# Eight of sixteen K tiles of an attention output projection's last two column blocks by seven products

## The chip, the cores and the metric

The kernel runs on one core of a Trainium2 chip. The metric is device time in microseconds (us) of one execution. The kernel before takes 2151.49 us (median of 3 runs, 2151.38 to 2151.53). All durations below come from one profiled execution of it.

## The reference, cut to what matters

The model is a two-layer encoder trunk over 256 positions of width 2048, float32 throughout. Layer 0 mixes by pooling and attention, layer 1 by an mLSTM, and each layer ends in a gated feed-forward network (FFN). The change touches only the output projection of layer 0:

```python
mixed = jnp.concatenate([pool_out, att_out], axis=-1) @ w_out_ab[e]   # (256, 2048) @ (2048, 2048)
x = x + mixed
x = x + conv_ffn(rms_norm(x, norm_ffn[layer]), ...)
```

The concatenation has 16 K tiles of 128 channels: 4 of pooling, then one for each of 12 heads. The next RMS norm needs all four 512-wide column blocks of `x`.

## The kernel before

**Precision.** Every float32 operand is held as a high part in the matmul's format (F32R) and a low part, the rest. A product is three matmuls: high by high, high by low, low by high. TensorE (PE) runs them all from `mm` (L296).

**The weight stream.** Weights arrive in chunks of 128 partitions by 1024 floats (512 KB), in one fixed order, `Stream`. A chunk is loaded by SyncE's DMA queue (SPq, L101) into one of seven raw buffers `w`. Then ScalarE (ACT) casts it to the high part (L167), and VectorE (DVE) subtracts to get the low part (L168). Both land in one of five buffers `hl`. `Stream.next` keeps loads up to six and splits up to three chunks ahead of the one that PE takes, in program order. Some chunks of the FFNs are first added up on DVE; their kind says how:

```python
    if kind == "sum":
        pin(add(r, r, l))          # L151
    ...
    if kind == "left":
        pin(add(l, l, r))          # L155
    if kind == "chain":
        pin(add(l, l, self.sum))   # L157
        pin(add(r, r, l))          # L158
```

`l` and `r` are the two 512-wide halves of the chunk. These additions are pinned in program order (`pin`), and `split` calls the additions of chunk i ahead of its cast, and those of chunk i + 1 right behind the subtraction of chunk i.

**The output projection.** `out_proj` accumulates each column block `b` (512 columns) in one pair of PSUM banks, for the two halves `t` of the positions. A chunk holds two K tiles of one column block and gives PE 12 matmuls of 512 columns: two K tiles, two halves, three terms. Blocks 0 and 1 run first, interleaved with the end of attention; blocks 2 and 3 then take 8 chunks each. `residual` (L470) adds a finished block into `x`, and `norm.add(b)` follows: squares on ACT (L369), four groups of four transposes on PE (`xt`, L347), and their scaled high and low parts on ACT (L359) and DVE (L362). The FFN's first products `up` need the last block's parts.

**Seven products elsewhere.** In the FFNs, groups of four column tiles already run as a Strassen-like scheme: seven products of sums of blocks in place of eight, in `quads`. There its chunks alternate with ordinary `up` and `dn` chunks.

**What sets the order.** PE's order is that of the program text, with small tasks woven in by an estimated clock (`Weave`). DVE, ACT and SPq are ordered at build time by a scheduler; engines then wait for each other by semaphores. Meanwhile `make_step` builds sums of weights for the FFN in DRAM (`G`), by DMAs that add, from SPq and GpSimd's queue (POOL); each step hangs on the number of a loaded chunk (`places`).

Of the kernel before, what the change touches and what calls it, by code (L numbers as in the profile page):

```python
# [9 lines left out]
F32 = mybir.dt.float32  # L10
# [6 lines left out]
P = 128  # L17
# [48 lines left out]
class Stream:  # L66
# [182 lines left out]
def trunk(ctx: ExitStack, tc: tile.TileContext, gx, xT, xn, call, catt, cml, weights, make, out):  # L249
# [45 lines left out]
    def mm(out_, lhsT, rhs, start, stop):  # L295
        pe.matmul(out_, lhsT, rhs, start=start, stop=stop, skip_group_check=True)  # L296
# [122 lines left out]
    def mov_part(ps, act, kts, first, last):  # L419
# [3 lines left out]
        for i, k in enumerate(kts):  # L423
# [9 lines left out]
            wv.tick(1.29)  # L433

    def mov_group(act, name, width=512, before=None, after=None):

        ps = mmp.tile([P, 2, 512 if width > 256 else width], F32, tag="mm", name=name)
        per = CH * P // width
        hl = None
        for k in range(KT):  # L440
            if k % per == 0:
                before and before(k)
                hl = st.next()
                after and after(k)
# [26 lines left out]

    def out_proj(cat, norm, name, parts, ready):

        pss = [mmp.tile([P, 2, 512], F32, tag="mm", name=f"op{name}_{i}") for i in range(2)]
        for i, kts in enumerate(parts):
            ready(i)
            for ps in pss:
                mov_part(ps, cat, kts, i == 0, i == len(parts) - 1)
        for b in range(NB):
            if b >= 2:  # L480
                ps = mmp.tile([P, 2, 512], F32, tag="mm", name=f"op{name}_{b}")
                mov_part(ps, cat, sum(parts, []), True, True)
            else:
                ps = pss[b]
            residual(ps, b)
            norm.add(b)


    def attention_layer(norm, nxt):
        with ExitStack() as es:  # L490
# [262 lines left out]
            need = [set(range(8)), {"pool0", "pool1"}, set(range(8, 12))]  # L753

            def ready(i):
                wv.until(lambda: need[i] <= done)

            out_proj(cat, nxt, "0", ATT_PARTS, ready)


# [212 lines left out]
    def ffn_layer(layer, norm, nxt):  # L973
        with ExitStack() as es:
# [64 lines left out]

            def product(bank, act, w, c, first, last):  # L1040

                (xh, xl), (wh, wl) = act, (w[:, j, c : c + 512] for j in range(2))
                mm(bank, xh, wh, first, False)
                mm(bank, xh, wl, False, False)
                mm(bank, xl, wh, False, last)
                wv.tick(0.68)

            def block_of(k, t):
# [173 lines left out]
def _mov(w):  # L1222

    return w.reshape(-1, 2, P, 512).transpose(0, 2, 1, 3).reshape(-1, P, CH * P)
# [256 lines left out]
```

## Time and profile before

| | |
|---|---|
| median of 3 runs | 2151.49 us |
| the profiled execution | 2151.58 us |
| its span, first to last instruction | 2149.8 us |
| TensorE clock granted | 1.0 |
| PE busy | 2143.8 us |
| DVE busy | 1792.6 us |
| ACT busy | 1335.6 us |
| DMA | 647.54 MB, mean 301 GB/s |

The span leaves 1.8 us of the profiled time around it. The part that the change touches is block 2 and block 3 of the projection, which PE works on from about 210 to 256 us after the span's start. A row of the timeline gives start and duration in us, engine, line, operation, the tile written, the tiles read, shapes and count; in brackets stands the idle time before it and what ended it. A busy PE row covers the pipeline's depth too, so the pace of matmuls is read from starts, not from the duration of one.

### The profile page before, as it was taken

What the parts mean: (1) busy time and instruction counts of PE and PEld (TensorE: products, weight loads), DVE (VectorE), ACT (ScalarE), POOL (GpSimd) and SP (SyncE); (2) the same over time, 40 slices, a digit from 0 to 9 for tenths busy, and PEclk for the clock granted to TensorE, in tenths of its full rate; (3) what the DMA queues carried; (4) which work ended last, traced back from release to release, by engine and by line L of the source; (5) the groups of instructions that cost most, each with busy time, mean ns of one, the idle gap of its engine ahead of it and who ended that gap; (6) DMA issues with size and microseconds to landing.
All of it is one profiled execution on the core that took longest, in us unless ns stands there. A gap on an engine that the chain in (4) does not pass through costs nothing.

```text
span 2149.8 us, 30986 instructions
## 1 busy us (share of the span) xinstructions
PE 2143.8 (100%) x10752; PEld 1813.8 (84%) x10752; DVE 1792.6 (83%) x2514; ACT 1335.6 (62%) x1872; POOL 243.6 (11%) x304
## 2 busy tenths in 40 slices
PE   9999999999999999999999999999999999999999
PEld 7888888888888888889888888888888888888887
DVE  7686698989889797877888887779898898988985
ACT  7665566766567576656455554456675776766863
POOL 0222111111111111100000011110111111100000
PEclk9999999999999999999999999999999999999999
DMA  9989899999999999968899999997999999988882
GB/s 355 253 225 256 252 252 358 308 340 322 304 328 316 349 325 338 322 178 278 349 339 327 334 303 333 313 319 216 346 317 333 341 335 323 350 291 263 289 271 98
DMA packets 213728, 647.54 MB, mean 301 GB/s; under 512 B 26586, under 2 KB 28930, under 8 KB 206914
## 3 DMA queue, kind: packets, MB, share of 16 engines
q1 hardware_dynamic: 181280, 590.68, 76.5%
q0 software_dynamic: 29216, 51.14, 15.1%
q10 hardware_dynamic: 3074, 3.75, 0.9%
q8 instruction: 84, 1.38, 0.3%
q14 instruction: 74, 0.61, 0.1%
HBM read 616.05 MB, written 131.12 MB: 348 GB/s over the span
## 4 chain that ended last, share of the span: by engine, by line
PE 97%; DVE 2%; issue 0%; DMA 0%; ACT 0%; ACTq 0%; DVEq 0%
PE dn L296 22%; PE p L296 21%; PE up L296 20%; PE op L296 8%; PE mk L296 4%; PE mq L296 4%; PE mo L296 4%; PE mv L296 4%; PE qproj L296 3%; PE kproj L296 1%; PE pool L296 1%; PE vproj L296 1%; PE tr L1118 1%; DVE hl L168 1%; PE qk L296 1%; PE end L296 1%
## 5 line engine op out<-in xcount | busy, mean ns | idle before, releaser
L168 DVE TENSOR_TENSOR hl<-w,hl 128x1024 fp32r<-128x1024 f32 (+1 forms) x916 | 1104.7, 1219 | 253.6 <-ACT hl L167 246.0
L167 ACT CAST hl<-w 128x1024 fp32r<-128x1024 f32 (+2 forms) x915 | 948.7, 1048 | 585.2 <-PE dn L296 113.3
L296 PE MATMUL dn<-hl,g 128*128 128x512 f32 x2064 | 491.5, 391 | 0.0
L296 PE MATMUL up<-xx,hl 128*128 128x512 f32 (+1 forms) x2560 | 466.5, 337 | 0.0
L296 PEld LDWEIGHTS up<-xx,hl 128*128 128x128 f32 x2560 | 405.0, 188 | 63.7
L296 PEld LDWEIGHTS dn<-hl,g 128*128 128x128 f32 x2064 | 385.2, 188 | 79.2
L296 PE MATMUL p<-hl,sx 128*128 128x512 f32 x1152 | 304.2, 390 | 0.2 <-DVE hl L168 0.2
L296 PEld LDWEIGHTS p<-hl,sx 128*128 128x128 f32 x1152 | 212.2, 188 | 42.1 <-DVE hl L168 0.5
L296 PE MATMUL p<-hl,xx 128*128 128x512 f32 x864 | 236.3, 391 | 0.0
L139 POOL DMA_DIRECT2D G<-in_q x140 | 118.4, 852 | 657.6 <-DMA G<-in_q 650.0
L296 PEld LDWEIGHTS p<-hl,xx 128*128 128x128 f32 x864 | 158.2, 188 | 30.1
L143 POOL DMA_DIRECT2D G<-G x124 | 108.2, 872 | 550.8 <-DMA G<-in_q 231.2
L296 PE MATMUL mv<-hl,xx 128*128 128x512 f32 (+2 forms) x480 | 92.4, 350 | 0.0
L296 PE MATMUL mq<-xx,hl 128*128 128x512 f32 (+1 forms) x512 | 91.9, 337 | 0.0
L296 PE MATMUL mk<-xx,hl 128*128 128x512 f32 (+1 forms) x512 | 91.8, 338 | 0.0
L296 PE MATMUL op<-hl,cat 128*128 128x512 f32 x384 | 91.6, 393 | 0.0
L296 PE MATMUL mo<-hl,xx 128*128 128x512 f32 x384 | 90.4, 391 | 0.0
L296 PE MATMUL op<-hl,mcat 128*128 128x512 f32 x384 | 89.7, 392 | 0.0
L296 PEld LDWEIGHTS mq<-xx,hl 128*128 128x128 f32 x512 | 79.2, 188 | 11.6
L296 PEld LDWEIGHTS mk<-xx,hl 128*128 128x128 f32 x512 | 78.8, 188 | 11.4
L296 PEld LDWEIGHTS mv<-hl,xx 128*128 128x128 f32 x480 | 78.1, 189 | 11.1
L296 PEld LDWEIGHTS op<-hl,mcat 128*128 128x128 f32 x384 | 71.4, 188 | 14.6
(250 smaller groups left out, 1939.5 us busy)
## 6 DMA issues: line engine op xcount, KB each, us to landing
w<-in_dn SPq DMA_DIRECT2D x176, 512.0 KB, 6.9
w<-in_up SPq DMA_DIRECT2D x160, 512.0 KB, 6.7
w<-in_m_in SPq DMA_DIRECT2D x124, 512.0 KB, 6.4
w<-G SPq DMA_DIRECT2D x88, 512.0 KB, 7.2
w<-in_q SPq DMA_DIRECT2D x80, 512.0 KB, 7.5
G<-in_q SPq DMA_DIRECT2D x124, 256.0 KB, 7.4
G<-G POOLq DMA_DIRECT2D x124, 256.0 KB, 7.7
w<-in_q SPq DMA_DIRECT2D x120, 256.0 KB, 6.2
```

The costliest lines, as they stand in the source:

```text
L139: pin(add.dma_start(G[r, 0:512], src[r, 512:1024], accum_op=ALU.add))
L143: pin(add.dma_start(G[:, at : at + 512], G[:, of : of + 512], accum_op=ALU.add))
L167: (self.nc.vector.tensor_copy if i + c == 0 else self.nc.scalar.copy)(hl[:, 0, c : c + n], w[:, c : c + n])
L168: self.nc.vector.tensor_sub(hl[:, 1, c : c + n], w[:, c : c + n], hl[:, 0, c : c + n].bitcast(F32))
L296: pe.matmul(out_, lhsT, rhs, start=start, stop=stop, skip_group_check=True)
L1118: pe.transpose(tr[:, j, t * P : t * P + P], src[:, c : c + P], ident)
```

## The change

K tiles 0 to 7 (pooling and heads 0 to 3) of column blocks 2 and 3 no longer go block by block. Four pairs of K tiles, two halves of positions and two column blocks form 2 by 2 block products, each done in seven products (`into`). Their seven results accumulate in four single PSUM banks (b1, b5, b6, b4) and are added straight into `x` by nine additions and one copy (L484 to L488, L496, L503 to L506 of the new program). K tiles 8 to 15 stay as they were.

- PE: 84 matmuls take the place of 96, all of 512 columns.
- The weights come as 4 "sum" and 4 "chain" chunks, 2 plain ones and 4 "left" ones, where 8 plain chunks were: 14 for 8. The 8 sum and chain chunks carry 6 matmuls each, the 2 plain ones 6 each, the 4 left ones 6 each.
- DVE and ACT: `cat_sums` forms the four sums of blocks of `cat` with their high and low parts, four times, in the buffers of `kt` and `vt`; it is queued once all heads are done or on their way.
- Order: block 2's other 8 tiles, its residual, then the 8 sum and chain chunks, one plain chunk of block 3, the rest of the seven products, `norm.add(2)`, and the last three chunks of block 3. So block 2's norm moves from ahead of block 3 to its middle.
- The steps of `make_step` from chunk 76 on shift by the six new chunks.

```diff
--- before.py
+++ after.py
@@ -432,6 +432,80 @@
                 mm(ps[:, t], xl, wh, False, last and i == n - 1)
             wv.tick(1.29)
 
+    def product(bank, act, w, c, first, last):
+
+        (xh, xl), (wh, wl) = act, (w[:, j, c : c + 512] for j in range(2))
+        mm(bank, xh, wh, first, False)
+        mm(bank, xh, wl, False, False)
+        mm(bank, xl, wh, False, last)
+        wv.tick(0.68)
+
+    def pair_sums(two, tv, raw, dst):
+
+        v.tensor_add(tv, two[:, :, 0, :].bitcast(F32), two[:, :, 1, :].bitcast(F32))
+        a11, a21, a12, a22 = (tv[:, k, t * P : t * P + P] for k in range(2) for t in range(2))
+        s1, s2, s3, s4 = (raw[:, j] for j in range(4))
+        v.tensor_sub(s1, a21, a22)
+        v.tensor_add(s3, a11, a21)
+        v.scalar_tensor_tensor(s2, s1, -1.0, a11, ALU.mult, ALU.subtract)
+        v.tensor_sub(s4, s3, a12)
+        v.tensor_sub(s4, s4, a22)
+        for js, hi, lo in dst:
+            a.copy(hi, raw[:, js])
+            v.tensor_sub(lo, raw[:, js], hi.bitcast(F32))
+
+    def into(b, two, sum_of, m, name, apart, room):
+
+        def xs(t, n):
+            return x[:, t, (b + n) * 512 : (b + n + 1) * 512]
+
+        def bank(j):
+            return psp.tile([P, 512], F32, tag="ps", name=f"h{j}_{name}", side=int(j in (1, 5)))
+
+        def block_of(k, t):
+            return [two(k // 2)[:, k % 2, i, t * P : t * P + P] for i in range(2)]
+
+        for q in range(2 * m):
+            p, second = (q % m, q >= m) if apart else (q // 2, q % 2)
+            ends = p == 0, p == m - 1
+            hl = st.next()
+            if not second:
+                if p == 0:
+                    b1, b5 = bank(1), bank(5)
+                product(b1, block_of(2 * p, 0), hl, 0, *ends)
+                product(b5, sum_of(0, p), hl, 512, *ends)
+            else:
+                if p == 0:
+                    b6, b4 = bank(6), bank(4)
+                product(b6, sum_of(1, p), hl, 0, *ends)
+                product(b4, block_of(2 * p + 1, 1), hl, 512, *ends)
+            if q == 2 * m - 1:
+                ca = room()
+                a.copy(ca, b1)
+                v.tensor_add(xs(1, 1), xs(1, 1), b5)
+                v.tensor_sub(xs(0, 1), xs(0, 1), b6)
+                v.tensor_add(xs(1, 0), xs(1, 0), b4)
+                v.tensor_sub(xs(0, 1), xs(0, 1), ca)
+            yield
+        for n in range(m // 2):
+            hl = st.next()
+            for e in range(2):
+                p = 2 * n + e
+                product(b1, block_of(2 * p + 1, 0), hl, e * 512, False, p == m - 1)
+            if n == m // 2 - 1:
+                v.tensor_add(xs(0, 0), xs(0, 0), b1)
+            yield
+        for p in range(m):
+            hl = st.next()
+            product(b6, sum_of(2, p), hl, 0, False, p == m - 1)
+            product(b5, sum_of(3, p), hl, 512, False, p == m - 1)
+            if p == m - 1:
+                v.tensor_add(ca, ca, b6)
+                v.tensor_sub(xs(0, 1), xs(0, 1), b5)
+                v.tensor_add(xs(1, 1), xs(1, 1), ca)
+                v.tensor_sub(xs(1, 0), xs(1, 0), ca)
+            yield
+
     def mov_group(act, name, width=512, before=None, after=None):
 
         ps = mmp.tile([P, 2, 512 if width > 256 else width], F32, tag="mm", name=name)
...
@@ -469,17 +543,33 @@
             xs = x[:, t, b * 512 : b * 512 + 512]
             v.tensor_add(xs, xs, ps[:, t])
 
-    def out_proj(cat, norm, name, parts, ready):
+    def out_proj(cat, norm, name, parts, ready, half=None):
 
         pss = [mmp.tile([P, 2, 512], F32, tag="mm", name=f"op{name}_{i}") for i in range(2)]
         for i, kts in enumerate(parts):
             ready(i)
             for ps in pss:
                 mov_part(ps, cat, kts, i == 0, i == len(parts) - 1)
+        rest = [k for k in sum(parts, []) if half is None or k >= 8]
         for b in range(NB):
             if b >= 2:
                 ps = mmp.tile([P, 2, 512], F32, tag="mm", name=f"op{name}_{b}")
-                mov_part(ps, cat, sum(parts, []), True, True)
+                if half is not None and b == 2:
+                    mov_part(ps, cat, rest, True, True)
+                    residual(ps, b)
+                    wv.until(lambda: norm.blocks == 2)
+                    unit = half()
+                    for _ in range(8):
+                        next(unit)
+                    continue
+                if half is not None:
+                    mov_part(ps, cat, rest[:2], True, False)
+                    for _ in unit:
+                        pass
+                    norm.add(2)
+                    mov_part(ps, cat, rest[2:], False, True)
+                else:
+                    mov_part(ps, cat, rest, True, True)
             else:
                 ps = pss[b]
             residual(ps, b)
...
@@ -752,10 +842,32 @@
                 wv.add(pool_group(stat_group(xx, list(range(KT)), f"pool{g2}"), g2))
             need = [set(range(8)), {"pool0", "pool1"}, set(range(8, 12))]
 
+            sx = []
+
+            def two(p):
+                return catb[0][:, 2 * p : 2 * p + 2]
+
+            def cat_sums():
+                sx.extend(kp.tile([P, 2, 4, 2, P], F32R, tag=tag, name=f"sx{tag}") for tag in ("kt", "vt"))
+                for p in range(4):
+                    tv = t1p.tile([P, 2, S], F32, tag="qt20", name=f"cs{p}")
+                    raw = tp.tile([P, 4, P], F32, tag="tb", name=f"cr{p}")
+                    pair_sums(two(p), tv, raw, [(slice(2 * i, 2 * i + 2), sx[i][:, :, p, 0], sx[i][:, :, p, 1])
+                                                for i in range(2)])
+                    yield 3.5
+                done.add("sums")
+
             def ready(i):
                 wv.until(lambda: need[i] <= done)
-
-            out_proj(cat, nxt, "0", ATT_PARTS, ready)
+                if i == 2:
+                    wv.add(cat_sums())
+
+            def half():
+                wv.until(lambda: "sums" in done)
+                return into(2, two, lambda j, p: [sx[j // 2][:, j % 2, p, i, :] for i in range(2)], 4, "op0", False,
+                            lambda: t1p.tile([P, 512], F32, tag="qt21", name="ca0"))
+
+            out_proj(cat, nxt, "0", ATT_PARTS, ready, half)
 
 
     def mlstm_layer(norm, nxt):
...
@@ -1234,12 +1338,23 @@
     return np.concatenate(out + [some(sum(parts, []), c) for c in range(1024, D, 512)])
 
 
+def _half_chunks(t):
+
+    t = t.reshape(-1, 2, P, 2, 512).transpose(0, 1, 3, 2, 4)
+    b11, b12, b21, b22 = (t[:, k, n] for k in range(2) for n in range(2))
+    return (np.concatenate([b11, b12, b22, b21], axis=2), np.concatenate([b21[0::2], b21[1::2]], axis=2))
+
+
 def _att_chunks(w_in, w_out):
     pool_w, q_w = 512, HEADS * HD
     cols = [pool_w + q_w, pool_w, pool_w + q_w + 512, pool_w + 512, pool_w + 1024]
     a = [_mov(w_in[:, c : c + 512]) for c in cols]
     a += [_stat(w_in[:, c : c + 256], range(KT)) for c in (0, 256)]
-    return np.concatenate(a), _out_chunks(w_out, ATT_PARTS)
+    out = _out_chunks(w_out, ATT_PARTS)[: 2 * KT // 2]
+    rest = [k for k in sum(ATT_PARTS, []) if k >= 8]
+    t = w_out.reshape(KT, P, D)
+    out = [out] + [_mov(t[rest][:, :, c : c + 512].reshape(len(rest) * P, 512)) for c in (1024, 1536)]
+    return np.concatenate(a), np.concatenate(out), *_half_chunks(t[:8][:, :, 1024:].reshape(8 * P, 1024))
 
 
 def _ml_chunks(w_in, w_out):
...
@@ -1458,11 +1573,14 @@
     n = 3 * (MD + 32)
     vg = [t["m_g"][:, c : min(c + n, m_g.shape[1])] for c in range(0, m_g.shape[1], n)]
     pairs = [_pairs(l, t[f"q{l}"]) for l in range(2)]
-    att, ml = chunks("a_in") + chunks("a_out"), vg + chunks("m_in") + chunks("m_out")
+    ao, four, last = (chunks(n) for n in ("a_out", "a_four", "a_last"))
+    ao = (ao[:20] + [e for q in four for e in (("sum", q[:, 0:1024]), ("chain", q[:, 1024:2048]))] + ao[20:21] + last
+          + [("left", q[:, 512:1536]) for q in four] + ao[21:])
+    att, ml = chunks("a_in") + ao, vg + chunks("m_in") + chunks("m_out")
     weights = att + ffn(0)
-    places = [[(24 + 13 * k // 2, 3) for k in range(8)] + [(76 + 9 * k, 4) for k in range(8)]
-              + [(150 + 4 * k, 2) for k in range(8)] + [(180 + 10 * k, 5) for k in range(8)]
-              + [(264 + 8 * k, 4) for k in range(8)]]
+    places = [[(24 + 13 * k // 2, 3) for k in range(8)] + [(82 + 9 * k, 4) for k in range(8)]
+              + [(156 + 4 * k, 2) for k in range(8)] + [(186 + 10 * k, 5) for k in range(8)]
+              + [(270 + 8 * k, 4) for k in range(8)]]
     at = len(weights) + len(ml)
     early = [(at - 240 + 11 * k, 5) for k in range(7)]
     late = [(at - 64 + 9 * k, 4) for k in range(7)]
```

The first place is DVE's queue where block 2 begins. `w` is a raw chunk, `hl` a split one, `x` the residual, `xx` the norm's parts, `op_2` block 2. Before:

```order
L168 TENSOR_TENSOR hl_2066<-w_2009,hl_2066 128x1024
L168 TENSOR_TENSOR hl_2083<-w_2026,hl_2083 128x1024
L470 TENSOR_TENSOR x<-x,op_0_1669 128x512 x2
L168 TENSOR_TENSOR hl_2105<-w_2044,hl_2105 128x1024
L168 TENSOR_TENSOR hl_2135<-w_2064,hl_2135 128x1024
L470 TENSOR_TENSOR x<-x,op_1_1670 128x512 x2
L168 TENSOR_TENSOR hl_2152<-w_2081,hl_2152 128x1024
L168 TENSOR_TENSOR hl_2191<-w_2098,hl_2191 128x1024
L362 SCALAR_TENSOR_TENSOR xx_131<-xt_0_2161,gcol,xx_131 128x256 x2
L168 TENSOR_TENSOR hl_2226<-w_2133,hl_2226 128x1024
```

Now, from the first summed chunk (hl_2203) on:

```order
L151 TENSOR_TENSOR w_2107<-w_2107 128x512
L544 TENSOR_TENSOR x<-x,op_1_1670 128x512 x2
L168 TENSOR_TENSOR hl_2203<-w_2107,hl_2203 128x1024
L157 TENSOR_TENSOR w_2124<-w_2124,w_2107 128x512
L158 TENSOR_TENSOR w_2124<-w_2124 128x512
L168 TENSOR_TENSOR hl_2244<-w_2124,hl_2244 128x1024
L151 TENSOR_TENSOR w_2171<-w_2171 128x512
L362 SCALAR_TENSOR_TENSOR xx_131<-xt_0_2214,gcol,xx_131 128x256
L362 SCALAR_TENSOR_TENSOR xx_131<-xt_2_2229,gcol,xx_131 128x256
L168 TENSOR_TENSOR hl_2271<-w_2171,hl_2271 128x1024
L157 TENSOR_TENSOR w_2201<-w_2201,w_2171 128x512
L362 SCALAR_TENSOR_TENSOR xx_131<-xt_0_2214,gcol,xx_131 128x256
```

Plain subtractions have become a sequence in which additions (L151, L157, L158) stand between one chunk's subtraction and the next.

The second place is DVE's queue at the four "left" chunks (hl_2413 to hl_2456), behind the last plain one (hl_2390), in the changed program:

```order
L168 TENSOR_TENSOR hl_2390<-w_2354,hl_2390 128x1024
L155 TENSOR_TENSOR w_2366<-w_2366 128x512
L488 TENSOR_TENSOR x<-x,ca_2400 128x512
L168 TENSOR_TENSOR hl_2413<-w_2366,hl_2413 128x1024
L155 TENSOR_TENSOR w_2377<-w_2377 128x512
L496 TENSOR_TENSOR x<-x,h_op_2305 128x512
L168 TENSOR_TENSOR hl_2431<-w_2377,hl_2431 128x1024
L155 TENSOR_TENSOR w_2388<-w_2388 128x512
L168 TENSOR_TENSOR hl_2443<-w_2388,hl_2443 128x1024
L155 TENSOR_TENSOR w_2407<-w_2407 128x512
L168 TENSOR_TENSOR hl_2456<-w_2407,hl_2456 128x1024
```

Each subtraction is followed by the next chunk's addition, which its own cast waits for.

The third place is PE's queue around block 2's transposes (`xt_8`, `xt_10`). Before, they stood in block 3's second chunk:

```order
L296 MATMUL op_2_2132<-hl_2226,cat_333 128x512 x12
L296 MATMUL op_2_2132<-hl_2243,cat_333 128x512 x12
L296 MATMUL op_3_2320<-hl_2261,cat_332 128x512 x12
L296 MATMUL op_3_2320<-hl_2282,cat_332 128x512 x6
L347 MATMUL xt_8_2350<-cst,x 128x128 x4
L296 MATMUL op_3_2320<-hl_2282,cat_332 128x512 x6
L347 MATMUL xt_10_2365<-cst,x 128x128 x4
L296 MATMUL op_3_2320<-hl_2299,cat_333 128x512 x12
L296 MATMUL op_3_2320<-hl_2324,cat_333 128x512 x12
```

Now they stand behind the seven products' last chunk (hl_2456), one and a half chunks on:

```order
L296 MATMUL h_op_2321<-hl_2456,sxvt 128x512 x3
L296 MATMUL h_op_2306<-hl_2456,sxvt 128x512 x3
L296 MATMUL op_3_2406<-hl_2470,cat_333 128x512 x12
L296 MATMUL op_3_2406<-hl_2481,cat_333 128x512 x6
L347 MATMUL xt_8_2538<-cst,x 128x128 x4
L296 MATMUL op_3_2406<-hl_2481,cat_333 128x512 x6
L347 MATMUL xt_10_2553<-cst,x 128x128 x4
L296 MATMUL op_3_2406<-hl_2492,cat_333 128x512 x12
```

And DVE's queue from that chunk's subtraction on, where `x` gets its last additions (L504 to L506), which these transposes read:

```order
L168 TENSOR_TENSOR hl_2456<-w_2407,hl_2456 128x1024
L168 TENSOR_TENSOR hl_2470<-w_2429,hl_2470 128x1024
L168 TENSOR_TENSOR hl_2481<-w_2441,hl_2481 128x1024
L503 TENSOR_TENSOR ca_2400<-ca_2400,h_op_2321 128x512
L504 TENSOR_TENSOR x<-x,h_op_2306 128x512
L168 TENSOR_TENSOR hl_2492<-w_2454,hl_2492 128x1024
L168 TENSOR_TENSOR hl_2511<-w_2465,hl_2511 128x1024
L505 TENSOR_TENSOR x<-x,ca_2400 128x512
L506 TENSOR_TENSOR x<-x,ca_2400 128x512
L168 TENSOR_TENSOR hl_2529<-w_2479,hl_2529 128x1024
```

The additions have two chunks' subtractions ahead of them on one side and two in their middle.

More of the change, by code (lines that the diff above doesn't have):

```diff
@@ L1038, in sums @@
                         yield 2.0
[L1040 to L1046, printed above, removed]
             def block_of(k, t):
@@ L1432 @@
     m_g = np.concatenate([wv0, wgate], axis=2).reshape(P, KT * (MD + 32))
-    a_in, a_out = _att_chunks(i["w_in_ab"][0], i["w_out_ab"][0])
+    a_in, a_out, a_four, a_last = _att_chunks(i["w_in_ab"][0], i["w_out_ab"][0])
     m_in, m_out = _ml_chunks(i["w_in_c"][0], i["w_out_c"][0])
@@ L1439 @@
         "call": call, "catt": catt, "cml": cml, "m_g": m_g,
-        "a_in": a_in, "a_out": a_out, "m_in": m_in, "m_out": m_out,
+        "a_in": a_in, "a_out": a_out, "a_four": a_four, "a_last": a_last, "m_in": m_in, "m_out": m_out,
     }
```

## The prediction

> **What bounds the kernel now.** I read the page's busy times and clock first, then the chain of work that ended last, then the stretch that is changed.
>
> ```profile
> span 2149.8 us, 30986 instructions
> PE 2143.8 (100%) x10752; PEld 1813.8 (84%) x10752; DVE 1792.6 (83%) x2514; ACT 1335.6 (62%) x1872; POOL 243.6 (11%) x304
> PEclk9999999999999999999999999999999999999999
> PE 97%; DVE 2%; issue 0%; DMA 0%; ACT 0%; ACTq 0%; DVEq 0%
> ```
>
> PE is busy throughout at the full granted clock, and 97% of the chain is PE. So a matmul removed is worth its time, if PE stays fed; DVE at 83% is the nearest rival. In the changed stretch the chain is PE alone:
>
> ```profile
> 199.91 14.06 PE op L296 x62
> 213.97 0.44 PE xt L347 x4
> 219.89 17.74 PE op L296 x78
> 239.88 16.38 PE op L296 x72
> ```
>
> ```profile
> L296 PE MATMUL op<-hl,cat 128*128 128x512 f32 x384 | 91.6, 393 | 0.0
> ```
>
> These are pieces of the chain by start, length and count. 16.38 / 72 is 0.2275 us a matmul, so a chunk of 12 takes 2.73 us and a chunk of 6 takes 1.36. No piece of another engine stands between. Four transposes take 0.44. By the group's row one matmul lasts 0.39 from start to end, so its end lies 0.17 behind the start of the next.
>
> What feeds PE is cast and subtraction. Two rounds of the timeline, ACT then DVE:
>
> ```profile
> 225.42 1.05 ACT L167 CAST hl<-w 128x1024 fp32r<-128x1024 f32 x1 [1.30 <-PE op L296]
> 226.51 1.22 DVE L168 TENSOR_TENSOR hl<-w,hl 128x1024 fp32r<-128x1024 f32 x1 [1.10 <-ACT hl L167]
> 228.18 1.05 ACT L167 CAST hl<-w 128x1024 fp32r<-128x1024 f32 x1 [1.71 <-PE op L296]
> 229.27 1.22 DVE L168 TENSOR_TENSOR hl<-w,hl 128x1024 fp32r<-128x1024 f32 x1 [1.54 <-ACT hl L167]
> ```
>
> The casts wait for PE to leave a buffer `hl`: splitting is as far ahead as five buffers allow, four chunks ready while a fifth is being made. From cast to subtraction takes 1.09 us (226.51 - 225.42), and both rest more than 1 us in each 2.76 us round. That rest is what the change can spend.
>
> **The saving.** 96 matmuls of 512 columns become 84 of the same shape. The products of the FFN, which have the new ones' form, run at the same pace:
>
> ```profile
> 2070.74 4.08 PE p L296 x18
> 2077.54 1.36 PE p L296 x6
> ```
>
> 4.08 / 18 is 0.2267. Twelve fewer matmuls save 12 x 0.227 = **2.7 us**.
>
> **What a summed chunk costs.** The one place of the trace with a "left" addition between two subtractions and nothing else on DVE:
>
> ```profile
> 496.15 1.23 DVE L168 TENSOR_TENSOR hl<-w,hl 128x1024 fp32r<-128x1024 f32 x1 [0.47 <-ACT hl L167]
> 497.30 0.69 DVE L155 TENSOR_TENSOR w<-w 128x512 f32<-128x512 f32 x1
> 498.15 1.05 ACT L167 CAST hl<-w 128x1024 fp32r<-128x1024 f32 x1 [2.03 <-DVE w L155]
> 499.23 1.23 DVE L168 TENSOR_TENSOR hl<-w,hl 128x1024 fp32r<-128x1024 f32 x1 [1.25 <-ACT hl L167]
> ```
>
> Subtraction, addition, cast and next subtraction form a closed chain, since additions are pinned right behind the subtraction before. From subtraction to subtraction it takes 499.23 - 496.15 = 3.08 us. A back-to-back subtraction frees DVE after 1.15 (497.30 - 496.15), and ACT starts 0.16 after the addition's end. A "sum" or "left" chunk thus takes 3.08 us to make. A "chain" chunk has a second addition that needs the first's result; the trace has no clean case, so I add one whole addition:
>
> ```profile
> L158 DVE TENSOR_TENSOR w<-w 128x512 f32<-128x512 f32 x8 | 5.5, 689 | 0.1
> ```
>
> That gives 3.08 + 0.69 = 3.77 us (between 3.68, if the two overlap as independent ones do, and 3.85, if a full 0.08 for the hand-over comes on top). PE uses such a chunk in 1.36 us. In the FFN 12 or 16 other matmuls follow each; here the eight stand in a row, and so do the four.
>
> **The eight sum and chain chunks.** Let t be the time since PE begins block 2. Then a fifth buffer comes free and chunk one is cast: 0.17 for PE's last matmul to end, 0.16 for the hand-over to ACT, 1.09 to the subtraction, which so starts at 1.4. Seven steps follow: four chain chunks and three sum chunks, 4 x 3.77 + 3 x 3.08 = 24.3. In that queue also stand eight parts of the norm and two residual additions:
>
> ```profile
> 218.06 2.05 DVE L362 SCALAR_TENSOR_TENSOR xx<-xt,gcol,xx 128x256 fp32r<-128x256 f32 x4
> 269.64 0.69 DVE L1030 SCALAR_TENSOR_TENSOR v<-v 128x512 f32<-128x512 f32 x1
> 270.24 0.69 DVE L1031 TENSOR_TENSOR v<-v 128x512 f32<-128x512 f32 x1
> ```
>
> They take 0.5 and 0.6 us each (2.05 / 4; 270.24 - 269.64). Where they lie in ACT's cast (1.2 us with its hand-over) they are free. Not so in the second chain chunk: three parts stand between its additions (1.5), and two parts and two additions behind them (2.2, of which 1.2 free). I take 1.9 of these 2.5, since the first of the parts runs while its own transposes are awaited. The last of the eight is subtracted from 1.4 + 24.3 + 1.9 = 27.6 to 28.8. PE could use it earlier: 48 matmuls of block 2 (10.9), 16 transposes (1.8), seven chunks (9.5) and the first matmul (0.2), together 22.4. So PE loses 28.8 - 22.4 = **6.4 us** there.
>
> **The four left chunks.** From the last chain subtraction's start, DVE has three more subtractions (with its own, 4 x 1.15), two additions into `x` (1.2), then addition, hand-over, cast and subtraction of the first left chunk (0.69 + 0.16 + 1.08 + 1.23): 9.0. (The two additions wait for nothing then.) PE, released 1.2 after that start, has 5 matmuls, 12 + 6 + 6 and one more, 29 x 0.227 = 6.6: it is there at 7.8 and loses 1.2. Each of the three others is made in 3.08 and used in 1.36: 1.7 lost, 5.2 together. Sum **6.4 us**.
>
> **Block 2's transposes.** The order puts them behind the last left chunk by 18 matmuls, and the two L506 additions that they need behind it by four subtractions and three additions. From the last left subtraction's start, DVE is done with these at 5 x 1.15 + 4 x 0.6 + 0.1 = 8.2; PE gets there at 1.2 + 23 x 0.227 = 6.4. Lost: **1.8 us**. What is late next is `xx` of block 2, which only `up` reads, 18 matmuls and block 3's transposes later; I cost that at nothing.
>
> **Sums of `cat`.** Four rounds on DVE, each one 512-wide addition (0.6), five 128-wide operations and two 256-wide ones:
>
> ```profile
> 262.79 0.47 DVE L388 TENSOR_SCALAR dg<-cst,re_n 128x128 f32<-128x128 f32 x2
> 150.00:178.00 28.00, 28.00 (x161) 24.40 (x161) 23.36 (x41) 20.28 (x46) 12.29 (x15) 1.00 0.85 207
> 178.00:190.00 12.00, 12.00 (x62) 10.10 (x61) 6.72 (x9) 5.45 (x8) 2.39 (x3) 1.00 0.95 232
> 178.00:256.30 78.30, 78.30 (x365) 65.01 (x364) 45.12 (x51) 39.51 (x56) 12.92 (x16) 1.00 0.92 264
> ```
>
> In these rows of stretches the fourth and fifth times are DVE's and ACT's. With 0.24 for a 128-wide operation (0.47 / 2) and 0.5 for a 256-wide one, a round is 0.6 + 1.2 + 1.0 = 2.8 us, 11 in all. From 178 to 190 DVE rests 5.3 us and from 190 to 205 again nearly half, so they hide. One risk: heads 10 and 11 still finish there, and a round ahead of their `pt` in DVE's queue holds up PE's `ov`. Between 0 and one round (2.8), I take **0.5**, near the free end, as rest is plenty.
>
> **Six more loads.** 6 x 0.524 MB = 3.1 MB.
>
> ```profile
> DMA packets 7499, 22.45 MB, mean 267 GB/s; under 512 B 1007, under 2 KB 1007, under 8 KB 7494
> q1 hardware_dynamic: 5702, 19.23, 67.5%
> ```
>
> Both rows are of the 84 us from 178 to 262. At 264 GB/s the 78.3 us before moved 20.7 MB; now 23.8 MB go in some 90 us, 264 GB/s again: the stalls themselves make the room. I take zero. If nothing hid them they would cost 3.1 x 0.675 x 84 / 19.23 = 9.3 us, the upper bound.
>
> **Sum.** -2.7 + 6.4 + 6.4 + 1.8 + 0.5 = **+12.4 us**. On the profiled execution's 2151.58 that is 2164.0; on the median, 0.1 lower, 2163.9. I forecast **2163.9 us**, slower. Its own uncertainty: 0.1 either way on each of ten steps, the parts' 1.9 (0 to 2.5), `cat` 0 to 2.8, which makes 2160.5 to 2167.8.
>
> **The rivals.**
> - *The work hides (faster).* If splitting ran far enough ahead, only the saving stayed: 2148.8. For it speaks the rest of over 1 us in each round. Against it: the head start is four chunks of 2.73, 10.9 us, and the eight lag by 7 x about 2.1. It decides where the eight are made in (28.8 - 6.4 - 4.5) / 7 = 2.6 us each or less, the left ones in 1.4. Chance 5%.
> - *Only busy time counts (no change).* DVE has 45.1 us in the 78.3; added are 16 additions (9.6), six subtractions (6.9), 11 for `cat`, nine additions into `x` (5.4): 78.0, against PE's 75.6. If queue order let DVE run dense, the stretch would take 78: 2151.2. Against it: the closed chain leaves DVE idle during each cast. Chance 5%.
> - *Half of it.* If the scheduler's order lets the eight chunks start earlier than I read, only left chunks and transposes count: -2.7 + 6.4 + 1.8 = +5.5, 2157.0. Chance 8%.
> - *Loads late.* SPq's additions into `G` share its queue; with the bound above, 2163.9 + 9.3 = 2173.2. Chance 9%.
> - *The clock falls.* In the left chunks PE would work 1.36 of 3.08 us. At half the clock six matmuls take 2.73, still under 3.08; up to block 3's end 36 matmuls could run slow, 36 x 0.227 = 8.2: between 2163.9 and 2172.1. Every clock digit of the page is 9, and no idle forecast is over 2.4 us (3.77 - 1.36). Chance 5%. The Trainium skill, "TensorE: Matmul & The Clock Gate", section "A second HAM failure mode: psum-queue depth-cycling", tells of a kernel whose frequent short idle gaps made the clock swing between half and full; no trace here has such gaps yet.
>
> The forecast has 68%. The range **2157 to 2170** holds it, half of the half case and part of the two slow ones. About 0.2%, 4.3 us, is what a measurement here can tell from no change. Faster by more, under 2147.2: 2%, as the hiding case is only 2.7 us under the median and a third of it may fall lower. Within: 11% (the other 3% of it, the busy-time case's 5%, and 3% of the half case, whose 2157.0 lies 1.2 over the bound of 2155.8). Slower: the remaining 87%.
>
> **What would show it.** Right: PE idle before single matmuls of the seven products, ended by DVE's L168 or ACT's L167; additions L155 and subtractions in a 3.1 us beat at the left chunks; an idle of about 2 us before `xt`; total about 15 us of PE idle between 205 and 270 us, none new later. Wrong: PE solid there (hiding); casts there that wait for DMA (loads); clock digits under 9. A wrong beat of the chain steps would move both 6.4 together.

## The result and the profile after

The changed kernel takes **2163.52 us** (median of 6 runs, 2162.92 to 2164.96) against 2151.51 for the kernel before, measured beside it: ratio 1.0056, 95% interval 1.0044 to 1.0067. It is 12.0 us slower; forecast were 12.4. Its profiled execution took 2164.96 us, with a span of 2163.1; the spans of its other runs are 1.3 to 2.0 us shorter.

The page of the changed kernel, the lines that answer to those of before:

```profile
span 2163.1 us, 31059 instructions
PE 2147.1 (99%) x10740; PEld 1813.3 (84%) x10740; DVE 1822.0 (84%) x2577; ACT 1343.2 (62%) x1887; POOL 243.8 (11%) x304
PEclk9999999999999999999999999999999999999999
PE 80%; DMA 3%; DVE 2%; issue 1%; ACT 1%; ACTq 0%; DVEq 0%; SPq 0%
```

The twelve matmuls are gone. The busy shares hardly moved, and the clock's 40 digits show nothing. The chain of waits could be followed back only to 262 us here, so its shares add up to 87% and do not compare with the 97% of before. The stretch has to be looked at by itself. Its end in that chain (start, length, count):

```profile
262.02 0.61 DVE x L506
262.68 0.55 PE xt L347 x3
...
267.83 3.47 PE up L296 x20
```

The chain of the kernel before had `up` here:

```profile
256.26 3.47 PE up L296 x20
```

`up` begins 11.57 us later, and the chain now comes to block 2's transposes through L506 on DVE. The first transposes of block 0, in the timelines of before and after:

```profile
213.81 0.60 PE L347 MATMUL xt<-cst,x 128*128 128x128 f32 x4
214.01 0.60 PE L347 MATMUL xt<-cst,x 128*128 128x128 f32 x4
```

They start 0.2 us later, a lag that PE has had since its first 28 us. So 11.4 us are lost between 214 and 268. PE's timeline there; the bracket is its idle time and who ended it:

```profile
226.45 1.61 PE L296 MATMUL h_op<-hl,cat 128*128 128x512 f32 x6 [1.56 <-DVE xx L362]
238.84 0.82 PE L296 MATMUL h_op<-hl,sxkt 128*128 128x512 f32 x2 [0.76 <-DVE hl L168]
249.59 1.43 PE L296 MATMUL h_op<-hl,sxvt 128*128 128x512 f32 x5 [0.70 <-DVE hl L168]
251.41 0.51 PE L296 MATMUL h_op<-hl,sxvt 128*128 128x512 f32 x1 [0.38 <-ACT hl L167]
252.67 1.42 PE L296 MATMUL h_op<-hl,sxvt 128*128 128x512 f32 x5 [0.76 <-DVE hl L168]
```

PE takes one matmul after the cast (L167), stops, and takes the next after the subtraction (L168), as forecast. The first row was not forecast: there PE waits 1.56 us until a transposes' reader (L362) frees the PSUM bank of product 4.

From start to start, beyond the pace of 0.227 us, PE lost 6.4 us at the eight chunks, 4.4 at the left ones and 1.5 at the transposes. A further 1.5 us is the clock. These are three stretches of 3.4 us around it (length, PE busy, granted clock, DMA share, GB/s):

```profile
232.50:235.92 3.42, 2.28 (x9) 1.00 0.47 159
235.92:239.33 3.41, 1.62 (x6) 1.00 0.42 156
239.33:242.74 3.41, 3.41 (x10) 0.50 0.82 239
```

For 3.41 us the granted clock was 0.50, right where PE could have worked without a pause. With the 2.7 us saved: 6.4 + 4.4 + 1.5 + 1.5 - 2.7 = 11.1 of the 11.4, and the rest are gaps too small to list.

By their mean granted clocks not every run has such a stretch: 0.999 here and in one other, which is what 3.41 us at half speed make of 2163 us, and 1.000 in four, which took 2162.9 to 2163.7 us, so the loss is nearly the same without it.

One larger wait came later, in this execution. At the mLSTM layer's output projection, DVE's queue (first row) waits for a DMA, and PE behind it (second):

```profile
1404.79 0.69 DVE L124 TENSOR_TENSOR gm<-gm 128x512 f32<-128x512 f32 x1 [6.61 <-DMA gm<-in_q]
1412.16 4.14 PE L296 MATMUL op<-hl,mcat 128*128 128x512 f32 x17 [0.98 <-DVE x L544]
```

PE lost 1.0 us there, which it had not before. Since the other runs' spans are 1.3 to 2.0 us shorter, this probably belongs to the profiled execution; the others have no trace to tell it from.

### The profile page after: what moved, and what is told of

It is laid out like the page before. It is cut to its first block, busy times and chain, and to the rows that moved or that the text cites. A ratio compares the mean times of both kernels' runs of the same rounds, so it can differ in the third digit from the quotient of the medians.

```text
span 2163.1 us, 31059 instructions
## 1 busy us (share of the span) xinstructions
PE 2147.1 (99%) x10740; PEld 1813.3 (84%) x10740; DVE 1822.0 (84%) x2577; ACT 1343.2 (62%) x1887; POOL 243.8 (11%) x304
## 4 chain that ended last, share of the span: by engine, by line
PE 80%; DMA 3%; DVE 2%; issue 1%; ACT 1%; ACTq 0%; DVEq 0%; SPq 0%
PE dn L296 22%; PE p L296 19%; PE up L296 18%; PE mk L296 4%; PE mq L296 4%; PE mo L296 4%; PE mv L296 4%; PE op L296 2%; DMA w<-G 1%; DVE hl L168 1%; PE tr L1222 1%; PE qk L296 1%; DMA w<-in_b 1%; PE end L296 1%; DMA gm<-in_q 1%
## 5 line engine op out<-in xcount | busy, mean ns | idle before, releaser
L167 ACT CAST hl<-w 128x1024 fp32r<-128x1024 f32 (+1 forms) x921 | 953.6, 1048 | 588.0 <-PE dn L296 108.0
L168 DVE TENSOR_TENSOR hl<-w,hl 128x1024 fp32r<-128x1024 f32 (+1 forms) x922 | 1110.4, 1218 | 242.4 <-ACT hl L167 235.3
L296 PEld LDWEIGHTS mk<-xx,hl 128*128 128x128 f32 x512 | 78.8, 188 | 11.4
L296 PEld LDWEIGHTS mo<-hl,xx 128*128 128x128 f32 x384 | 71.0, 188 | 14.2
```

The lines of the kernel that those rows point to most:

```text
L167: (self.nc.vector.tensor_copy if i + c == 0 else self.nc.scalar.copy)(hl[:, 0, c : c + n], w[:, c : c + n])
L168: self.nc.vector.tensor_sub(hl[:, 1, c : c + n], w[:, c : c + n], hl[:, 0, c : c + n].bitcast(F32))
```

## The experiments

The theory is the prediction's: a summed chunk passes from DVE (addition) to ACT (cast) and back to DVE (subtraction), and this closed chain, not the engines' busy time, makes PE wait. All variants start from the changed kernel; in some of them line numbers lie a few lines on (L168 is L170 or L171 there).

**1. No additions at all.** The three kinds of summed chunks become plain ones:

```diff
-ao = (ao[:20] + [e for q in four for e in (("sum", q[:, 0:1024]), ("chain", q[:, 1024:2048]))] + ao[20:21] + last
-      + [("left", q[:, 512:1536]) for q in four] + ao[21:])
+ao = (ao[:20] + [e for q in four for e in (q[:, 0:1024], q[:, 1024:2048])] + ao[20:21] + last
+      + [q[:, 512:1536] for q in four] + ao[21:])
```

> The twelve additions on the projection's sum, chain and left weight chunks are left out, so the products take unsummed weights and the output is not the reference's; loads, casts, subtractions, matmuls, sums of cat and residual additions stay. Theory (a closed chain of pinned addition, cast and subtraction sets the pace of summed chunks): a chunk is then made at DVE's pace of 1.15 us, under PE's 1.36, so the 6.4 us of the eight chunks and the 6 us of the left ones go; what may stay is the 1.7 us in which the fourth bank waits for block 1's last norm parts, and up to 1.5 at the transposes: 2150 to 2152.5 us, some 12 under the changed kernel. Rival, six more loads are late: they are still there, so 2160 or more. Rival, DVE's busy time alone: 16 additions of 0.6 us less, 2154.

Measured: 2150.58 us, ratio 0.9996 (0.9986 to 1.0005). The additions are 16 of DVE's 2577 instructions (4 + 8 + 4; the expectation counts twelve), and they carry the whole loss. The loads are the same, so these cost nothing. The matmuls' 2.7 us do not all appear: by the medians 1.05 us do, and the interval includes no change. PE waits for a PSUM bank here too, a chunk earlier, for product 5's:

```profile
224.40 1.63 PE L296 MATMUL h_op<-hl,sxkt 128*128 128x512 f32 x6 [1.19 <-DVE xx L362]
```

**2. The left addition twice.** One more addition of the same length in each left chunk:

```diff
 pin(add(l, l, r))
+if 48 <= i < 86:
+    pin(add(l, l, r))
```

> The addition of each of the four left chunks is done twice, one right behind the other (the output is not the reference's, since the second one adds once more). Theory: the four steps of the closed chain grow by one dependent addition, 0.73 us each, and PE waits on at least three of them in full: +2.2 to +2.9 on the changed kernel's 2163.5, so 2165.7 to 2166.4. Rival, DVE's rest hides additions, what binds is something else (loads, the queue of additions into x): DVE rests 1.25 us ahead of each of these subtractions, so no change, 2163.5.

Measured: 2167.81 us, ratio 1.0075 (1.006 to 1.009). It is slower, as the theory has it, but by 4.3 us where 2.2 to 2.9 were expected. The trace has the chain's part and another:

```profile
251.63 0.50 PE L298 MATMUL h_op<-hl,sxvt 128*128 128x512 f32 x1 [1.09 <-ACT hl L169]
256.69 3.33 PE L298 MATMUL h_op<-hl,sxvt 128*128 128x512 f32 x6 [0.47 <-DVE hl L170]
```

The wait for the cast grew from 0.38 to 1.09 us. In the second row six matmuls take 3.33 us, a short wait included, where six take 1.6 in a row at full clock: from 253.6 to 263.8 the clock was at 0.50. Longer stalls came with a longer stretch of half speed. From start to start, the slow matmuls cost 3.8 us here and 1.5 in the changed kernel, which is about the rest.

**3. The left addition a chunk earlier.** The next left chunk's addition is queued ahead of this chunk's subtraction, so it runs on DVE while ACT casts:

```diff
+if 48 <= i < 86 and i + 1 in self.w and self.w[i + 1][3] in ("left",):
+    self.sums(i + 1)
 self.nc.vector.tensor_sub(hl[:, 1, c : c + n], w[:, c : c + n], hl[:, 0, c : c + n].bitcast(F32))
```

> Same work; only at the four left chunks the addition of the next chunk is queued ahead of a chunk's subtraction, in ACT's cast, and no more behind it. Theory: the chain is open, a left chunk is made in DVE's 0.6 + 1.15 = 1.75 us in place of 3.08; against PE's 1.36 the four lose about 1 + 3 x 0.4 = 2.2 in place of 5.9 to 6.4: 2159.3 to 2160.0. Rival (DVE's busy time or loads bind there): the same work, no change, 2163.5.

Measured: 2159.63 us, ratio 1.0037 (1.0024 to 1.005), inside the expected 2159.3 to 2160.0. Not one instruction is added or removed, only the order changed, and 3.9 us came back. At the four left chunks PE now waits once, for 0.33 us:

```profile
249.76 4.54 PE L298 MATMUL h_op<-hl,sxvt 128*128 128x512 f32 x17 [0.33 <-DVE hl L170]
```

So at the left chunks it is the order of the chain that costs, not its work.

**4. The same at the eight.** `("left",)` becomes `("sum", "chain", "left")`.

> The same at the eight sum and chain chunks too. Theory: at the left chunks as in the run with those alone, -3.5 to -4.2. At the eight chunks a pair would take DVE 3 x 0.6 + 2 x 1.15 = 4.1 us in place of 6.85, but ten other DVE operations (4.4 us) stand among them in a queue that waits for PE's transposes, and DVE is then nearly full: I expect 1 to 4 of the 6.4 us back. Together 2155.5 to 2159.0. Rival (busy time binds at the eight): only the left part, 2159.5 to 2160. Rival (neither): 2163.5.

Measured: 2161.28 us, ratio 1.0045 (1.0028 to 1.0062). The theory expected 2155.5 to 2159.0: missed, there was no gain at the eight. DVE and ACT there:

```profile
229.25 1.22 DVE L170 TENSOR_TENSOR hl<-w,hl 128x1024 fp32r<-128x1024 f32 x1
230.39 0.69 DVE L151 TENSOR_TENSOR w<-w 128x512 f32<-128x512 f32 x1
230.99 0.69 DVE L158 TENSOR_TENSOR w<-w 128x512 f32<-128x512 f32 x1
231.84 1.99 ACT L167 CAST hl<-w 128x1024 fp32r<-128x1024 f32 x2 [3.42 <-DVE w L158]
237.41 0.69 DVE L487 TENSOR_TENSOR x<-x,h_op 128x512 f32<-128x512 f32 x1 [0.92 <-PE h_op L298]
```

The chain chunk's second addition (L158) landed behind the other chunk's subtraction and the next sum, so ACT casts two chunks at once and DVE waits for it. And at 237.41 an addition into `x`, which waits for PE, stands ahead of a subtraction that PE needs. The edit tested its own order rather than the theory; it decides nothing on the eight. The result lies nearest the rival in which busy time binds there (2159.5 to 2160), but DVE was busy for only 19.0 of the 24 us from 218 to 242.

**5 and 6. One stage alone.** In 5 only the left chunks are made plain, in 6 only the eight.

> Left out: the four additions of the left chunks (block 21 minus block 22 stays unsummed there, so this part of the output is not the reference's); the additions of the eight sum and chain chunks stay. Theory (each stage waits for its own chunks and the waits add up): without any addition the program took 2150.6; the eight chunks add the 6.4 us of PE waits that the changed kernel showed there, less the 1.4 to 1.7 us wait for the transposes' PSUM bank that is also there without additions: 2155.3, and 2156.8 where the clock's half speed of 3.4 us comes too. The wait before block 2's transposes goes with the left chunks. Rival (only the last wait on the way counts, so the left chunks are the whole loss): 2150.5 to 2152. Rival (the left chunks cost nothing of their own): 2163.5.

> Left out: the twelve additions of the eight sum and chain chunks (so the four products' weights there are unsummed and the output is not the reference's); the four additions of the left chunks stay. Theory (the left chunks' beat of 3.1 us against 1.36 us of PE work, and a lead of one to two chunks that the eight no longer use up): 2150.6 plus 3 x 1.7, less a lead of 0 to 2.7, plus 0 to 1.5 before block 2's transposes: 2153.0 to 2157.2. Rival (the two stages do not touch each other, so the left chunks and the transposes cost the prediction's full 8.2): 2158.8. Rival (the eight are the whole loss): 2150.5 to 2152.

Measured: 5, with the eight's additions only, 2158.25 us (ratio 1.0032, 1.002 to 1.0045), 1.4 us above what was expected; 6, with the left ones only, 2155.94 us (1.002, 1.0011 to 1.0029), within. Over the version without additions that is 7.7 and 5.4, together 13.0; both additions together cost 2163.5 - 2150.6 = 12.9. So by their totals the two stages add up, and neither is the whole loss. Kernel 5 first, then kernel 6:

```profile
246.84 5.60 PE L296 MATMUL h_op<-hl,sxvt 128*128 128x512 f32 x24
256.99 0.55 PE L347 MATMUL xt<-cst,x 128*128 128x128 f32 x3 [0.35 <-DVE x L506]
```

```profile
244.54 1.43 PE L296 MATMUL h_op<-hl,sxvt 128*128 128x512 f32 x5 [0.76 <-DVE hl L168]
254.55 0.55 PE L347 MATMUL xt<-cst,x 128*128 128x128 f32 x3 [1.35 <-DVE x L506]
```

In 5 the four left chunks run without a gap. The clock was at half speed for 3.41 us behind the eight, which the expectation's upper figure holds. It left out the transposes, which still wait (0.5 us from start to start); the other 0.9 us are not accounted for. In 6 the first left chunks run free on the lead that the eight had not used up; the trace has no half speed at all in that stretch.

**7. Cast and subtraction in halves.** The direct test of the chain: the work stays, the hand-overs overlap.

```diff
-w, n, width = self.w.pop(i)[:3]
+w, n, width, kind = self.w.pop(i)[:4]
+if 48 <= i < 86 and kind in ("sum", "chain", "left"):
+    n //= 2
```

> The cast and the subtraction of each summed chunk are done in two halves of 512 columns, so the subtraction of the first half runs while ACT casts the second; same arithmetic. Theory (the beat is a chain of hand-overs: addition, cast, subtraction, one after the other): a left chunk's beat falls from 3.08 to about 2.5 us (0.60 addition, 0.16, half a cast 0.53, two half subtractions 1.2), a chain chunk's from 3.71 to about 2.6: a gain of 3 to 6 us, 2157.5 to 2160.5; less where the queue of DVE puts an addition to x, which waits for PE, ahead of a subtraction. Rival (DVE's busy time is the bound there): 12 more subtractions at some 0.06 us more each, 2163.5 to 2164.5.

Measured: 2155.07 us, ratio 1.0017 (1.0008 to 1.0026). DVE and ACT have 12 more instructions each, and 8.4 of the 12 us are back, more than the 3 to 6 that were expected. PE's waits in the seven products are now three, of which the first is for product 4's bank:

```profile
226.60 1.63 PE L298 MATMUL h_op<-hl,cat 128*128 128x512 f32 x6 [1.77 <-DVE xx L364]
236.41 0.73 PE L298 MATMUL h_op<-hl,cat 128*128 128x512 f32 x2 [1.14 <-DVE hl L170]
245.96 2.81 PE L298 MATMUL h_op<-hl,sxvt 128*128 128x512 f32 x11 [0.40 <-DVE hl L170]
```

The rival, which has busy time as the bound, falls for the changed kernel. DVE's busy time is the more telling figure: the stretches from 218 us to about the end of the last additions into `x`, of the changed kernel and of this one (length, then busy PE, PEld, DVE, ACT, POOL, granted clock, DMA share, GB/s):

```profile
218.00:262.00 44.00, 35.50 (x141) 25.82 (x139) 36.19 (x46) 21.71 (x28) 4.04 (x5) 0.96 0.75 225
```

```profile
218.00:254.00 36.00, 31.66 (x139) 24.66 (x138) 35.44 (x56) 21.86 (x34) 2.94 (x4) 1.00 0.85 259
```

In the changed kernel DVE is busy 36 of 44 us, in this one 35.4 of 36. Now busy time is the bound: with its hand-overs hidden, DVE has nothing left to give there.

**8. The left additions on POOL.** POOL is busy 11% of the time. It does the additions, queued up to two chunks ahead:

```diff
-pin(add(l, l, r))
+pin((self.nc.gpsimd.tensor_add if 48 <= i < 86 else add)(l, l, r))
...
+for k in (i + 1, i + 2):
+    if 48 <= i < 86 and k in self.w and self.w[k][3] == "left":
+        self.sums(k)
```

> The four additions of the left chunks are done by POOL, queued up to two chunks ahead, instead of DVE; same arithmetic. Theory (the addition on DVE is what makes the left chunks' beat): the left chunks' subtractions follow each other in about 1.2 us, so the left chunks' 4.4 us and up to 1.5 before block 2's transposes come back: 2157.6 to 2159.2. Estimate of POOL's price from its 128x256 additions of 0.85 to 1.2 us: 1.7 to 2.4 us each, ahead of need. Rival (POOL's queue stands behind its DMA additions, each of which waits some us for a load, or POOL's reads hold up DVE's): the sums come later than DVE would have had them, 2163.5 to 2172.

Measured: 2164.09 us, ratio 1.0056 (1.0043 to 1.0069). No gain. The left chunks do run without a gap, yet the time went elsewhere:

```profile
235.85 1.81 POOL L155 TENSOR_TENSOR w<-w 128x512 f32<-128x512 f32 x1 [1.02 <-issue]
236.54 1.66 DVE L158 TENSOR_TENSOR w<-w 128x512 f32<-128x512 f32 x1
246.24 3.40 DVE L491 TENSOR_TENSOR x<-x,ca 128x512 f32<-128x512 f32 x1
246.28 2.80 POOL L155 TENSOR_TENSOR w<-w 128x512 f32<-128x512 f32 x2
249.64 5.60 PE L299 MATMUL h_op<-hl,sxvt 128*128 128x512 f32 x24
```

An addition on DVE that lasts 0.69 us takes 1.66 and 3.40 beside POOL's, and ends 0.5 to 0.6 us after these. So DVE is held up until POOL is done, with both operands of both in SBUF; one addition (L157) that DVE began at 235.83, just ahead of POOL's, took its usual 0.68. The Trainium skill, "SBUF — State Buffer", section "SBUF: two separate sides", states this: a DVE operation with two SBUF inputs and a POOL operation that reads SBUF share a pair of ports, and one blocks the other for its full length. The trace agrees. The stalls moved: at the chain chunks two waits are now 1.60 and 2.00 us (0.76 and 1.03 in the changed kernel), block 2's transposes wait 2.34 (1.32), and the clock was at half for 6.8 and once more for 3.4 us.

**9 and 10. Toward a version that pays.** What was left in the halves' version were four waits of PE: the three above and 1.15 us before block 2's transposes. In 9 products 6 and 4 lie in the halves of one tile of the plain products' PSUM, the transposes are queued 1.5 us later by `Weave`'s clock, and a chain chunk ahead of a plain one is cast whole. In 10, besides, block 3's first plain chunk stands in the middle of the eight.

```diff
+if 48 <= i < 86 and kind in ("sum", "chain", "left") and (
+        kind != "chain" or isinstance(self.srcs[i + 1], tuple)):
+    n //= 2
...
+def pair():
+    both = mmp.tile([P, 2, 512], F32, tag="mm", name=f"h64_{name}")
+    return both[:, 0], both[:, 1]
...
-b6, b4 = bank(6), bank(4)
+b6, b4 = pair() if name == "op0" else (bank(6), bank(4))
...
-norm.add(2)
+norm.add(2, 4.5)
```

```diff
-for _ in range(8):
+for _ in range(4):
     next(unit)
+ps3 = mmp.tile([P, 2, 512], F32, tag="mm", name=f"op{name}_3")
+mov_part(ps3, cat, rest[:2], True, False)
+for _ in range(4):
+    next(unit)
```

> Halves as before, but not for the chain chunk ahead of a plain one; products 6 and 4 accumulate in the two halves of one of the plain products' PSUM tiles, so that no bank of theirs has to be freed by the transposes' readers first; block 2's transposes are queued one and a half products' ticks later. Same arithmetic. Theory (what is left in the version with halves are four separate waits of PE: 1.9 us for the PSUM bank, 1.3 at the last chain chunk, 0.6 at a left chunk, 1.3 before the transposes, which add up): the bank's, the transposes' and most of the last chain chunk's come back, 2155.1 - 3.2 to 4.5 = 2150.6 to 2151.9, about the kernel before. Rival (DVE, with its additions, has too little time there, and a wait that is taken away turns up at the next chunk): 2153.5 to 2155.5.

> As the version with the two PSUM halves and the delay, and block 3's first plain chunk (2.7 us of PE work for 1.2 us of DVE work) is multiplied between the fourth and the fifth of the eight summed chunks instead of behind them. Same arithmetic. Theory (the lead of the casts over PE is what hides the additions, and a plain chunk in the middle rebuilds 1.5 us of it): 2149.5 to 2151.5, at best under the kernel before by the 2.7 us of matmuls saved less 0.7 of waits. Rival (the waits are already gone without it, so the place of the plain chunk does not matter): within 0.5 us of the version that is not interleaved. Rival (the plain chunk only takes the wait from the later four chunks to the left ones): 2152 to 2154.

Measured: 9 takes 2157.8 us (ratio 1.0027, 1.0017 to 1.0036), 10 takes 2159.06 (1.0033, 1.0021 to 1.0045): both slower than the halves alone, and over even the rivals' figures. Kernel 9, then 10:

```profile
233.58 0.50 PE L299 MATMUL h_op<-hl,sxkt 128*128 128x512 f32 x1 [1.02 <-ACT hl L170]
270.72 0.67 PE L299 MATMUL npr<-dg,cst 128*128 128x256 f32 x2 [2.19 <-DVE dg L391]
```

```profile
242.34 2.17 PE L299 MATMUL h_op<-hl,sxvt 128*128 128x512 f32 x7 [1.21 <-DVE x L494]
245.26 1.66 PE L299 MATMUL h_op<-hl,sxvt 128*128 128x512 f32 x6 [0.76 <-DVE hl L171]
```

The bank's wait and the transposes' wait are gone, and others stand in their place. At the last chain chunk, which is cast whole again, PE in 9 waits 1.02 us for the cast and then 0.76 for the subtraction, where the halves' version waits 1.14. At the norm's end (`npr`) 2.19 us are new in both; the halves' version, with its earlier transposes, has no wait there. All nine runs of 9 also have a mean clock of 0.998 or 0.999, and its trace has 3.41 us at half speed. In 10 product 6 has to wait for L494, which reads product 4 from the tile that they now share. Since 9 changes three things at once, what each is worth is not shown. That waits taken away turned up elsewhere agrees with a DVE that is full (experiment 7). No version that computes the same beats the kernel before.

## Why the prediction was right

The number was right, 2163.9 against 2163.5, and its theory held: experiments 1, 3 and 7 speak for it, 2 and 6 agree, 4 decides nothing. That the two figures lie only 0.4 us apart is partly luck. Three terms of the sum were too large, by 2.8 us together; what made that up in the profiled execution, the clock and the later losses, was not in the sum, and the other runs have no trace that would tell how it came out there. By its own steps:

- *The saving, 2.7 us.* The 12 matmuls are gone. Without additions only 1.05 us of it shows (experiment 1), since a bank's wait of 1.2 to 1.4 us comes with the new products.
- *What a summed chunk costs.* The row from the FFN gave the right beat. Subtractions on DVE in the changed kernel:

```profile
211.49 1.22 DVE L168 TENSOR_TENSOR hl<-w,hl 128x1024 fp32r<-128x1024 f32 x1
215.20 1.23 DVE L168 TENSOR_TENSOR hl<-w,hl 128x1024 fp32r<-128x1024 f32 x1 [1.16 <-ACT hl L167]
...
237.56 3.50 DVE L168 TENSOR_TENSOR hl<-w,hl 128x1024 fp32r<-128x1024 f32 x3 [0.28 <-ACT hl L167]
...
245.24 1.23 DVE L168 TENSOR_TENSOR hl<-w,hl 128x1024 fp32r<-128x1024 f32 x1 [0.65 <-ACT hl L167]
...
248.31 1.23 DVE L168 TENSOR_TENSOR hl<-w,hl 128x1024 fp32r<-128x1024 f32 x1 [0.27 <-ACT hl L167]
...
254.46 3.50 DVE L168 TENSOR_TENSOR hl<-w,hl 128x1024 fp32r<-128x1024 f32 x3 [1.24 <-ACT hl L167]
```

  A left chunk takes 248.31 - 245.24 = 3.07 us (3.08 forecast), a chain chunk 215.20 - 211.49 = 3.71 (3.77).
- *The eight chunks, 6.4 us.* From the first of their subtractions to the last, 211.49 to 237.56, are 26.1 us; forecast were 26.2. PE lost 6.4. The PSUM bank's wait of 1.6 us was not foreseen and lies inside this. DVE went on with its chain meanwhile, so a PE that had not waited there would have met the same late subtractions; experiment 9, without that wait, agrees, but no run tests it alone.
- *The left chunks, 6.4 us.* Mis-sized: 4.4. The first left chunk was to lose 1.2 (1.0, since the matmuls that it lists add up to 30 and not 29) and lost nothing: PE came to it at 247.15, 0.7 us behind its subtraction's end (245.24 + 1.23). Half the clock had cost PE 1.5 us ahead of that. Coming late also left less to wait for at the three others, 4.4 in place of 5.2.
- *The clock.* A rival at 5%, told as an extra of up to 8.2 us. It did fall in the profiled execution, for 3.41 us, and mostly took the place of a wait that was forecast. So the sum hardly moved: 4.4 + 1.5 against 6.4. Four of the six runs did without it and were as slow. The sign named for it, clock digits under 9, could not show it, since a digit averages over 54 us.
- *Block 2's transposes, 1.8 us.* Measured 1.5. The L506 additions ended 8.2 us after the last left subtraction began (262.63 - 254.46), as forecast. Experiment 5 shows that they are late because of the left additions: without these, the loss is 0.5 from start to start.
- *Sums of `cat`, 0.5 us.* Measured nothing: the first transposes, behind the sums, start 0.2 us late, and PE had that lag long before. The cost of *six more loads*, zero, was right too (experiment 1).
- *Nothing new later.* Not quite: 1.0 us at the mLSTM layer, probably of the profiled execution alone.

Of the rivals, "only busy time counts" fell for the changed kernel, yet it is what the halves' version runs into, 3.5 us above the kernel before, where the rival had put it at no change.

## What to carry to other kernels

When work is added to an engine that is 83% busy, ask first whether the added operation stands between two engines' hand-overs: the closed chain from DVE to ACT and back cost 3.1 us for 1.75 us of DVE work, and a change of order (at four chunks) or of piece size (at all twelve) alone brought back 3.9 and 8.4 of 12 us. Then take the engine's busy time in that very stretch, since it is what stays when the chain is broken. And an idle engine is no free helper if it shares what the busy one needs: POOL's additions stopped DVE's.

## What the runs showed of the hardware

The granted clock went to 0.50 in steps of 3.41 us (3.41, 6.83 or 10.24). These begin on a grid that counts from the clock's first record, which lies at 4.4 to 7.2 us in these traces, and PE need not be idle for it. Counting PE's busy share in each such stretch between 222 and 270 us, in the changed kernel and nine variants: of the eleven full-clock stretches with 52% or less, nine were followed by half speed; of those with 54% or more, none. Two of the changed kernel's six runs have such a stretch by their mean clock; that the place of the grid decides which is likely, but not shown. The rows of 235.92 (1.62 of 3.41, then 0.50) and 232.50 (2.28 of 3.42, then 1.00) are one of each. One that did not fall, from the halves' version:

```profile
224.30:227.70 3.40, 1.63 (x8) 1.00 0.79 145
```

The edge of one half is a count over few stretches, with matmul ends that are modelled, and not a law. The Trainium skill, "TensorE: Matmul & The Clock Gate", section "Part 1: The HAM clock gate", has the window of 3413 ns, running free of the kernel, and the two speeds; the trace agrees. That section asks for an idle window before half speed, and there the trace differs: a window that was 48% busy was enough. The Trainium skill, "TensorE: Matmul & The Clock Gate", section "A second HAM failure mode: psum-queue depth-cycling", named in the prediction, tells of short gaps that swing the clock; the runs here show that, with gaps of 0.4 to 2.3 us.
